# Up products of the first feed-forward read through 21 ways of laying out and addressing their operands

## The chip, the cores and the metric

The kernel runs on one core of a Trainium2 chip. The metric is the device time of one execution in microseconds, the median of several runs. Everything below on single instructions comes from one profiled execution of the kernel before.

## What is computed

A two-layer trunk over 256 tokens of width 2048. Layer 0 is differential attention and a gated feed-forward with a causal convolution; layer 1 is a gated DeltaNet and the same kind of feed-forward. The change touches the up products of the first feed-forward and, beside them, the two products in which the weights are the moving operand (the values of the attention, the gate z of the DeltaNet):

```python
def conv_ffn(h, w_up, conv_w, conv_b, w_down):
    u = causal_dwconv(h @ w_up, conv_w) + conv_b
    val, gate = jnp.split(u, 2, axis=-1)
    return (jax.nn.silu(gate) * val) @ w_down

for i in range(DEPTH):
    h = rms_norm(x, mixer_norm[i])
    x = x + (diff_attention(h, ...) if i % 2 == 0 else gated_deltanet(h, ...))
    x = x + conv_ffn(rms_norm(x, ffn_norm[i]), ffn_w_up[i], ffn_conv_w[i], ffn_conv_b[i], ffn_w_down[i])
```

`h @ w_up` is 256 x 2048 by 2048 x 11008, that is 43 blocks of 128 value and 128 gate columns.

## The kernel before, in words

All activations lie with features on the 128 partitions and tokens along the free dimension. A float32 number is carried as the sum of two float32r numbers, hi and lo, and a product is made of three: hi by hi, lo by hi, hi by lo. These are lines 115, 116 and 117 in `dense`. Each is one matmul with its own load of 128 x 128 weights; the activations move (256 columns), the weights stand still. `dense` makes one tile of 2 x 128 output features over all of the input features: 16 groups of 128 input features, two output halves (c), three products, which is 96 matmuls for a tile of 16 groups. The weights come in chunks of four groups: `weights` issues a DMA of 512 KB on SP (line 88), ScalarE rounds the chunk to float32r (line 89, tile `whi`), and VectorE takes the rest (line 90, tile `wlo`). `raw`, `whi` and `wlo` have three buffers each.

Where the operands lie matters to this text. `whi` and `wlo` have room for 128 columns more than they hold, and `weights` starts them `d` columns into that room. The activations stand at known places modulo 128 columns (512 bytes of a partition): the normed input `h` at 40, the feed-forward's inner activations `ac` at 48, the DeltaNet's `oc` at 112 (HP, AP, OP). `dense` passes d = (place - 45) mod 128, so that in every one of its products the weights stand 45 columns behind the activations modulo 128. Chunks, groups and halves are multiples of 128 columns, so they keep this distance.

`dense_tok` (line 139) turns the roles round: the activations are loaded as weights (128 tokens), the weight tile moves, 256 columns at a time, and d = (40 + 45) mod 128 keeps the same distance. It serves the attention's values (`w_v`, 4 calls) and the DeltaNet's z (`w_z`, 8 calls), with 192 matmuls a call.

Order of the work: attention, first feed-forward (43 up tiles in `ffn`, line 262, then the down products in `project`), DeltaNet, second feed-forward. Small products of the attention and the DeltaNet (lines 226, 475 to 658) are put between the chunks of the large ones. Each engine works through its queue in program order, and what waits for what is set by the tiles.

Of the kernel before, what the change touches and what calls it, by code (L numbers as in the profile page):

```python
# [16 lines left out]
P = 128  # L17
T = 256
D = 2048
KD = D // P  # L20
EPS = 1e-6
CK = 4
GAP = 45
HP, AP, OP = 40, 48, 112
LNEXP = "natural_log_exp_and_others"


class Trunk:
# [69 lines left out]
    def banks(self):  # L98
        return self.dps.tile([P, 2, 2 * T], F32, tag="ps", name="ps")

    def dense(self, w, kt, acts, place, tiles=2, lead=0):

        nc = self.nc
        ps = self.banks()
        for k0, nk in self.chunks(kt, CK, lead):
            hi, lo = self.weights(w[:, k0:k0 + nk, :], (place - GAP) % P)
            steps = [(k, c) for k in range(nk) for c in range(tiles)]
            if k0 + nk == kt:
                steps = [(k, c) for c in range(tiles) for k in range(nk)]
            for k, c in steps:  # L110
                a = acts(k0 + k)
                first, last = k0 + k == 0, k0 + k == kt - 1
                s = slice(c * P, (c + 1) * P)
                o = ps[:, c, :T]
                nc.tensor.matmul(o, hi[:, k, s], a[:, 0, :], start=first, stop=False)  # L115
                nc.tensor.matmul(o, lo[:, k, s], a[:, 0, :], start=False, stop=False)  # L116
                nc.tensor.matmul(o, hi[:, k, s], a[:, 1, :], start=False, stop=last)  # L117
            self.tick()
        return ps

# [1 line left out]

        self.nc.vector.tensor_tensor(u, ps[:, :, :T], self.rstd.unsqueeze(1).to_broadcast([P, 2, T]), ALU.mult)

    def dense_tok(self, w, kt, acts):

        nc = self.nc
        ps = self.banks()
        for k0, nk in self.chunks(kt, CK // 2):
            hi, lo = self.weights(w[:, k0:k0 + nk, :], (HP + GAP) % P)  # L130
            for k in range(nk):
                a = acts(k0 + k)
                first, last = k0 + k == 0, k0 + k == kt - 1
                for c in range(2):
                    ah, al = (a[:, i, c * P:(c + 1) * P] for i in range(2))
                    halves = [slice(i * T, (i + 1) * T) for i in range(2)]
                    for j, (l, r) in enumerate(((ah, hi), (ah, lo), (al, hi))):
                        for i, s in enumerate(halves):
                            nc.tensor.matmul(ps[:, c, s], l, r[:, k, s],  # L139
                                             start=first and not (i or j), stop=last and i + j == 3)  # L140
            self.tick()
        return ps
# [108 lines left out]
    def ffn(self, w_up, w_down, nj, cols_ap, done, final=False):  # L251

        nc = self.nc
        self.spawn(self.norm_stat())
        with self.tc.tile_pool(name="fp", bufs=1) as fp:
            cols = fp.tile([P, 8 * nj + 64], F32, tag="fcols", name="fcols")[:, :8 * nj]
            cols = cols.rearrange("p (t h j) -> p t h j", t=4, h=2)
            nc.scalar.dma_start(cols, cols_ap)
            acts = []
            rows = self.rows(fp.tile([P, nj * 2 * T + 8], F32R, tag="ac", name="ac"), nj, 0)  # L260
            for j in range(nj):
                ps = self.dense(w_up[j], KD, self.h_acts, HP)
                c = []
                u = fp.tile([P, 2, T], F32, tag="u", name="u", bufs=2)
                self.merge(ps, u)
                for half in range(2):
                    o = fp.tile([P, T], F32, tag=f"cv{half}", name="cv", bufs=2)
                    c4 = [cols[:, t, half, j:j + 1] for t in range(4)]
                    self.conv(o, u[:, half, :], c4[:3], c4[3])
                    c.append(o)  # L270
                nc.scalar.activation(c[1], c[1], AF.Silu)
                a = c[0]
                nc.vector.tensor_tensor(a, c[0], c[1], ALU.mult)
                ac = rows[j]
                self.split(ac, a)
                acts.append(ac)
            self.project(w_down, nj, lambda k: acts[k], AP, done, final)

    def attention(self, w_qk, w_v, w_o, nh, dist_ap, ident_ap, qg, kg, lvec, sub, start, done, lambda_init):

        nc, mp = self.nc, self.mp
        with self.tc.tile_pool(name="at", bufs=1) as at:
# [107 lines left out]
            for h in range(nh):  # L390
                acts, lead = (self.h_acts, 0) if h else (start, 1)
# [4 lines left out]
                self.spawn(weigh(h, qn, kn, go, aT))  # L396
                aTs.append(aT)
            for h in range(0, nh, 2):
                pv = self.dense_tok(w_v[h // 2], KD, self.h_acts)
                v = at.tile([P, 2, 2 * T], F32, tag="v", name="v", bufs=2)  # L400
                for c in range(2):
                    nc.scalar.mul(v[:, c, :], pv[:, c, :], self.rstdc[:, c:c + 1])
                for i in range(2):
                    self.spawn(values(h + i, v[:, :, i * T:(i + 1) * T], aTs[h + i]))
# [7 lines left out]
    def gdn(self, w_gate, w_in, w_z, w_out, nb, hb, gate_ap, const_ap, hot_ap, conv_col, ng, done):  # L412
# [7 lines left out]
        nc, tc, mp = self.nc, self.tc, self.mp  # L420
# [4 lines left out]
        with tc.tile_pool(name="gd", bufs=1) as gd:  # L425
# [25 lines left out]
            def convs(u, tiles):  # L451
                c = gd.tile([P, 2, T], F32, tag="cv", name="cv", bufs=4)
                for i in range(2):
                    self.conv(c[:, i, :], u[:, i, :], [conv_col(t, tiles[i]) for t in range(4)], None)
                nc.scalar.activation(c, c, AF.Silu)  # L455
                return c
# [213 lines left out]
            for b in range(nb):  # L670
                heads = range(b * hb, (b + 1) * hb)
                cc = gd.tile([P, 32, 32], F32, tag="s4", name="Cc", bufs=3)
                nc.gpsimd.memset(cc, 0.0)
                lqs, inv, acts, zts, vts = [], [], [], {}, {}
                groups = [range(i, i + gh) for i in range(0, hb, gh)]
                plan = [("k", i) for i in range(hb)] + [("v", 0)] + [("z", g) for g in range(len(groups))]
                for op, i in plan + [("v", i) for i in range(1, hb)]:
                    if op == "k":
                        hq = heads[i]
                        c = convs(lin(self.dense(w_in[hq * 2], KD, self.h_acts, HP)), (hq, nq + hq))  # L680
                        self.spawn(keys(hq, c, cc, 2 * i, lqs))
                        if i == hb - 1:
                            self.spawn(invert(cc, lqs, inv))
                    elif op == "z":
                        gr = groups[i]
                        zt = zts[i] = gd.tile([P, 2, gv, P], F32, tag="vz", name="zt", bufs=4)
                        ps = self.dense_tok(w_z[heads[gr[0]] // 2], KD, self.h_acts)
                        for t in range(2):
                            nc.scalar.activation(zt[:, t].rearrange(flat), ps[:, t, :], AF.Silu,
                                                 scale=self.rstdc[:, t:t + 1])  # L690
                    else:
                        gi = i // gh
                        gr = groups[gi]
                        if i == gr[0]:
                            vt = gd.tile([P, 2, gv, P], F32, tag="vz", name="vt", bufs=4)
                            ready = []
                            self.spawn(group(gi, gr, lqs, inv, vt, ready, zts, acts))
                        hq = heads[i]
                        c = convs(lin(self.dense(w_in[hq * 2 + 1], KD, self.h_acts, HP)),
                                  (2 * nq + 2 * hq, 2 * nq + 2 * hq + 1))  # L700
                        self.spawn(to_tokens(c, vt, 2 * (i - gr[0]), ready))
                if pend:
                    out(*pend)
                pend = (b, acts)
# [59 lines left out]
NJ = 43  # L764
# [5 lines left out]
def _tiles(a):  # L770

    return a.reshape(-1, P).T


def _layout(inputs):
# [3 lines left out]
    x = {k: np.asarray(v) for k, v in inputs.items()}  # L779
# [9 lines left out]
    def blocks(w, kt, starts):  # L789
        w = w.reshape(kt, P, -1)  # L790
        return np.stack([np.concatenate([w[:, :, a:a + n] for a, n in s], 2) for s in starts]).transpose(0, 2, 1, 3)

    def pairs(n):
        return [[(T * i, T)] for i in range(n)]
# [8 lines left out]
    up = [[(j * P, P), (ff + j * P, P)] for j in range(NJ)]  # L803
    q, k = np.arange(P)[:, None], np.arange(T)[None]
    dist = []
    for t, n in ((0, P), (1, T)):
# [3 lines left out]
    i = np.arange(P)  # L810
# [3 lines left out]
    fcols = [  # L814
        np.concatenate([_tiles(x["ffn_conv_w"][i].reshape(-1)), _tiles(x["ffn_conv_b"][i])], 1).reshape(P, 4, 2, NJ)
        for i in range(2)]
    out = {
        "x": x["x"][0].T.reshape(KD, P, T).transpose(1, 0, 2),
        "cols": np.concatenate(col, 1),
# [3 lines left out]
        "dist": np.concatenate(dist, 1),  # L823
        "fcols0": fcols[0],
        "fcols1": fcols[1],
        "w_up0": blocks(x["ffn_w_up"][0], KD, up),
        "w_down0": blocks(x["ffn_w_down"][0], NJ, pairs(D // T)),
        "w_gate": np.pad(wi[:, 2 * kd + 2 * vd:], ((0, 0), (0, P - 2 * NV))).reshape(KD, P, P).transpose(1, 0, 2),
        "w_in": blocks(wi, KD, gin),
# [78 lines left out]
```

## Time and profile before

| what | value |
|---|---|
| median of 3 runs | 2676.85 us (2675.2 to 2677.72) |
| the profiled execution: its own time | 2676.33 us |
| the profiled execution: span from first to last instruction | 2674.6 us |
| TensorE matmul busy | 2656.4 us, 99% of the span |
| VectorE, ScalarE, GpSimd busy | 69%, 54%, 4% |
| granted TensorE clock, mean | 0.999 |
| DMA | 481.77 MB, mean 180 GB/s |
| up products of the first feed-forward | from 405 to 874 us of the span |

How to read it: a matmul's row in the trace gives its start and a modelled duration of about 278 ns, in which the next two matmuls already start. The pace of TensorE is therefore not read from the duration but from start to start, or from the number of matmuls in a stretch of time. That pace is called the spacing below.

### The profile page before, as it was taken

To read this page: it belongs to the slowest core of one execution; us is meant where nothing else is said; L and a number is where in the kernel's file an instruction comes from. 1 tells how busy PE (TensorE), PEld (TensorE's weight loads), DVE (VectorE), ACT (ScalarE), POOL (GpSimd) and SP (SyncE) were. 2 spreads that over 40 slices of the span, in tenths; PEclk is the share of its full clock that TensorE was granted. 3 is DMA by queue.
4 is the path that set the end of the run, shared out by engine and by line. 5 is a ranking of instruction groups with operands and counts; after the bars stand their busy time and mean duration, and the time that the engine had idled before them with its cause. 6 is when DMAs were issued, how large, how long until landed. Compare 5 with 4: busy or idle time off the path is not lost.

```text
span 2674.6 us, 55978 instructions
## 1 busy us (share of the span) xinstructions
PE 2656.4 (99%) x23504; PEld 2639.4 (99%) x23504; DVE 1845.2 (69%) x2719; ACT 1453.3 (54%) x1994; POOL 112.1 (4%) x221
## 2 busy tenths in 40 slices
PE   8999999999999999999999999999999999999999
PEld 8999999999999999999999999999999999999999
DVE  7775567777777555688787687688677777776444
ACT  6555555555555444584764664574565555554333
POOL 0000000000000000031011021021000000000000
PEclk9999999999999999999999999999999999999999
DMA  6555566666666666655355454555466666666765
GB/s 205 172 174 164 159 192 194 195 195 193 195 193 195 193 194 192 190 156 177 115 170 166 143 169 155 157 159 174 143 194 195 194 193 196 193 195 197 203 200 165
DMA packets 135469, 481.77 MB, mean 180 GB/s; under 512 B 15408, under 2 KB 18480, under 8 KB 135216
## 3 DMA queue, kind: packets, MB, share of 16 engines
q1 hardware_dynamic: 134064, 475.58, 58.6%
q8 instruction: 184, 3.01, 0.5%
q10 hardware_dynamic: 1152, 2.61, 0.3%
q14 instruction: 69, 0.57, 0.1%
HBM read 476.03 MB, written 2.10 MB: 179 GB/s over the span
## 4 chain that ended last, share of the span: by engine, by line
PE 93%; DVE 3%; ACT 3%; issue 1%; DMA 1%; ACTq 0%; DVEq 0%; SPq 0%
PE ps L115 26%; PE ps L116 26%; PE ps L117 26%; PE ps L139 10%; PE mp L610 2%; DVE wlo L90 1%; ACT whi L89 1%; PE mp L226 1%; DVE cv L207 1%; ACT L455 0%; PE mp L574 0%; PE mp L580 0%; DMA raw<-w_in 0%; PE mp L589 0%; PE mp L498 0%
## 5 line engine op out<-in xcount | busy, mean ns | idle before, releaser
L90 DVE TENSOR_TENSOR wlo<-raw,whi 128x1024 fp32r<-128x1024 f32 (+2 forms) x909 | 1105.2, 1217 | 660.9 <-ACT whi L89 659.8
L89 ACT CAST whi<-raw 128x1024 fp32r<-128x1024 f32 (+2 forms) x909 | 948.6, 1044 | 1034.8 <-PE ps L117 830.8
L115 PE MATMUL ps<-h,whi 128*128 128x256 f32 x4304 | 1195.0, 278 | 7.8 <-ACT h L152 5.6
L116 PE MATMUL ps<-h,wlo 128*128 128x256 f32 x4304 | 1194.8, 278 | 4.4 <-DVE wlo L90 4.4
L117 PE MATMUL ps<-h,whi 128*128 128x256 f32 x4304 | 1193.7, 277 | 0.0
L115 PEld LDWEIGHTS ps<-h,whi 128*128 128x128 f32 x4304 | 809.4, 188 | 9.8 <-ACT h L152 5.6
L116 PEld LDWEIGHTS ps<-h,wlo 128*128 128x128 f32 x4304 | 809.8, 188 | 7.7 <-DVE wlo L90 5.9
L117 PEld LDWEIGHTS ps<-h,whi 128*128 128x128 f32 x4304 | 810.0, 188 | 0.6
L115 PE MATMUL ps<-ac,whi 128*128 128x256 f32 x1632 | 450.4, 276 | 0.0
L116 PE MATMUL ps<-ac,wlo 128*128 128x256 f32 x1632 | 450.3, 276 | 0.0
L117 PE MATMUL ps<-ac,whi 128*128 128x256 f32 x1632 | 450.2, 276 | 0.0
L115 PEld LDWEIGHTS ps<-ac,whi 128*128 128x128 f32 x1632 | 306.2, 188 | 0.0
L116 PEld LDWEIGHTS ps<-ac,wlo 128*128 128x128 f32 x1632 | 306.2, 188 | 0.0
L117 PEld LDWEIGHTS ps<-ac,whi 128*128 128x128 f32 x1632 | 306.2, 188 | 0.0
L139 PE MATMUL ps<-whi,h 128*128 128x256 f32 x1536 | 251.1, 284 | 0.0
L139 PEld LDWEIGHTS ps<-whi,h 128*128 128x128 f32 x1536 | 213.5, 190 | 0.2
L139 PE MATMUL ps<-wlo,h 128*128 128x256 f32 x768 | 155.7, 284 | 1.0 <-DVE wlo L90 1.0
L115 PE MATMUL ps<-oc,whi 128*128 128x256 f32 x512 | 143.9, 281 | 0.0
L207 DVE SCALAR_TENSOR_TENSOR cv<-u,fcols,cv 128x255 f32<-128x255 f32 (+1 forms) x344 | 142.8, 477 | 0.0
L117 PE MATMUL ps<-oc,whi 128*128 128x256 f32 x512 | 142.5, 278 | 0.0
L116 PE MATMUL ps<-oc,wlo 128*128 128x256 f32 x512 | 142.3, 278 | 0.0
L139 PEld LDWEIGHTS ps<-wlo,h 128*128 128x128 f32 x768 | 119.4, 190 | 2.0 <-DVE wlo L90 1.4
(201 smaller groups left out, 2048.7 us busy)
## 6 DMA issues: line engine op xcount, KB each, us to landing
raw<-w_up SPq DMA_DIRECT2D x344, 512.0 KB, 4.3
raw<-w_down SPq DMA_DIRECT2D x160, 512.0 KB, 4.1
raw<-w_in SPq DMA_DIRECT2D x128, 512.0 KB, 4.1
raw<-w_z SPq DMA_DIRECT2D x64, 512.0 KB, 4.4
raw<-w_out SPq DMA_DIRECT2D x64, 512.0 KB, 3.9
raw<-w_qk SPq DMA_DIRECT2D x63, 512.0 KB, 4.0
raw<-w_v SPq DMA_DIRECT2D x32, 512.0 KB, 3.7
raw<-w_o SPq DMA_DIRECT2D x32, 512.0 KB, 4.1
```

The costliest lines, as they stand in the source:

```text
L89: nc.scalar.copy(hi, raw)
L90: nc.vector.tensor_tensor(lo, raw, hi.bitcast(F32), ALU.subtract)
L115: nc.tensor.matmul(o, hi[:, k, s], a[:, 0, :], start=first, stop=False)
L116: nc.tensor.matmul(o, lo[:, k, s], a[:, 0, :], start=False, stop=False)
L117: nc.tensor.matmul(o, hi[:, k, s], a[:, 1, :], start=False, stop=last)
L139: nc.tensor.matmul(ps[:, c, s], l, r[:, k, s], start=first and not (i or j), stop=last and i + j == 3)
L207: nc.vector.scalar_tensor_tensor(out[:, j:], u[:, :T - j], taps[n - 1 - j], out[:, j:], ALU.mult, ALU.add)
L226: last = self.nc.tensor.matmul(out, self.onesr, p[:, j], start=i + j == 0, stop=i + j == n)
L610: nc.tensor.matmul(p[:, v, :], l(v), r[:, v, :], start=i == 0, stop=i == len(terms) - 1)
```

## The change

Nothing is added to or taken from any engine's queue: the changed program has the same instructions in the same order on every engine, with the same waits and the same bytes moved. What changes is where in memory some operands stand and in which order a matmul reads and writes their columns.

A table WAYS of 21 triples (unit, back, shift) is used in the first feed-forward alone; up tile j takes entry j mod 21.

- unit 1: the two halves of a weight tile are interleaved, column by column, when the input is laid out on the host. The load of half c then reads every second column (step of two columns, 8 bytes), 128 of 256.
- back 1: the moving activations are read from the last column to the first, and the output is written to PSUM from the last column to the first, so that the result is the same.
- shift: the weights start that many columns further on, so that their distance to the activations changes.

The entries are (0,0,0) once, (1,1,16i) and (1,0,16i) for i from 0 to 7, and (0,1,32i) for i from 0 to 3. Of the 43 tiles 3 keep (0,0,0), 16 are interleaved and backwards, 16 interleaved alone, 8 backwards alone.

In `dense_tok` the moving weights are shifted too: by 0, 11, 22 and 33 columns in the four calls of the values, and by 44, 55 and so on to 121 in the eight calls of z. One of these 12 calls keeps its place.

```diff
+WAYS = [(0, 0, 0)] + [(1, 1, 16 * i) for i in range(8)] + [(1, 0, 16 * i) for i in range(8)] + [
+    (0, 1, 32 * i) for i in range(4)]
...
-    def dense(self, w, kt, acts, place, tiles=2, lead=0):
+    def dense(self, w, kt, acts, place, tiles=2, lead=0, way=(0, 0, 0)):
...
+        unit, back, shift = way
+
+        def cols(t, k, c):
+            if not unit:
+                return t[:, k, c * P:(c + 1) * P]
+            return t[:, k, :].rearrange("p (g c u) -> p c g u", c=2, u=unit)[:, c]
+
+        def turn(t):
+            return t[:, ::-1] if back else t
+
         for k0, nk in self.chunks(kt, CK, lead):
-            hi, lo = self.weights(w[:, k0:k0 + nk, :], (place - GAP) % P)
+            hi, lo = self.weights(w[:, k0:k0 + nk, :], (place - GAP + shift) % P)
...
-                s = slice(c * P, (c + 1) * P)
-                o = ps[:, c, :T]
-                nc.tensor.matmul(o, hi[:, k, s], a[:, 0, :], start=first, stop=False)
-                nc.tensor.matmul(o, lo[:, k, s], a[:, 0, :], start=False, stop=False)
-                nc.tensor.matmul(o, hi[:, k, s], a[:, 1, :], start=False, stop=last)
+                o = turn(ps[:, c, :T])
+                nc.tensor.matmul(o, cols(hi, k, c), turn(a[:, 0, :]), start=first, stop=False)
+                nc.tensor.matmul(o, cols(lo, k, c), turn(a[:, 0, :]), start=False, stop=False)
+                nc.tensor.matmul(o, cols(hi, k, c), turn(a[:, 1, :]), start=False, stop=last)
...
-    def dense_tok(self, w, kt, acts):
+    def dense_tok(self, w, kt, acts, shift):
...
-            hi, lo = self.weights(w[:, k0:k0 + nk, :], (HP + GAP) % P)
+            hi, lo = self.weights(w[:, k0:k0 + nk, :], (HP + GAP + shift) % P)
...
-                ps = self.dense(w_up[j], KD, self.h_acts, HP)
+                ps = self.dense(w_up[j], KD, self.h_acts, HP, way=WAYS[j % len(WAYS)] if not final else WAYS[0])
...
-                pv = self.dense_tok(w_v[h // 2], KD, self.h_acts)
+                pv = self.dense_tok(w_v[h // 2], KD, self.h_acts, 11 * (h // 2))
...
-                        ps = self.dense_tok(w_z[heads[gr[0]] // 2], KD, self.h_acts)
+                        ps = self.dense_tok(w_z[heads[gr[0]] // 2], KD, self.h_acts, 44 + 11 * (heads[gr[0]] // 2))
...
+    ups = blocks(x["ffn_w_up"][0], KD, up)
+    for j in range(NJ):
+        u = WAYS[j % len(WAYS)][0]
+        if u:
+            ups[j] = ups[j].reshape(P, KD, 2, P // u, u).swapaxes(2, 3).reshape(P, KD, T)
...
-        "w_up0": blocks(x["ffn_w_up"][0], KD, up),
+        "w_up0": ups,
```

## The prediction

> **What bounds the kernel now.** I read the page first, its line of busy shares and the chain that ended last.
>
> ```profile
> PE 2656.4 (99%) x23504; PEld 2639.4 (99%) x23504; DVE 1845.2 (69%) x2719; ACT 1453.3 (54%) x1994; POOL 112.1 (4%) x221
> ...
> PE 93%; DVE 3%; ACT 3%; issue 1%; DMA 1%; ACTq 0%; DVEq 0%; SPq 0%
> PE ps L115 26%; PE ps L116 26%; PE ps L117 26%; PE ps L139 10%; PE mp L610 2%; DVE wlo L90 1%; ACT whi L89 1%; PE mp L226 1%; DVE cv L207 1%; ACT L455 0%; PE mp L574 0%; PE mp L580 0%; DMA raw<-w_in 0%; PE mp L589 0%; PE mp L498 0%
> ```
>
> TensorE has 93% of the chain, and nearly all of it is the four lines that the change touches. Next I read the groups of instructions in the stretch of the first feed-forward's up products alone, to see whether anything else could end last there.
>
> ```profile
> L116 PE MATMUL ps<-h,wlo 128*128 128x256 f32 x1376 | 379.9, 276 | 0.0
> ...
> L90 DVE TENSOR_TENSOR wlo<-raw,whi 128x1024 fp32r<-128x1024 f32 x172 | 210.8, 1226 | 114.9 <-ACT whi L89 114.9
> L89 ACT CAST whi<-raw 128x1024 fp32r<-128x1024 f32 x172 | 181.0, 1052 | 202.6 <-PE ps L117 173.1 <-ACT cv L205 26.6 <-DMA raw<-w_up 2.9
> ```
>
> The matmuls have no idle time before them (0.0). ScalarE, which makes the weight chunks, stands idle for 202.6 us, 173.1 of these waiting for matmuls to free a buffer; only 2.9 us are put down to the DMA. So the supply of weights is ahead, and the stage lasts exactly as long as its matmuls. The table of stretches gives their pace (us, then PE busy and its count, PEld, DVE, ACT, POOL):
>
> ```profile
> 405.20:873.90 468.70, 468.70 (x4136) 468.65 (x4135) 334.83 (x476) 256.65 (x347) 0.00 (x0) 1.00 0.64 194
> ```
>
> 468.70 us over 4136 matmuls is 113.3 ns each, at a granted clock of 1.00. This is the number that everything hangs on: a matmul moves 256 columns, and while it does, the 128 columns of the next weights are loaded. The timeline of TensorE shows that the same products, with the same three lines and the same distance between their operands, have another pace elsewhere. First a piece of this stage, then one of the DeltaNet's input products, then the products with moving weights:
>
> ```profile
> 499.76 0.28 PE L116 MATMUL ps<-h,wlo 128*128 128x256 f32 x1
> ...
> 500.44 0.28 PE L116 MATMUL ps<-h,wlo 128*128 128x256 f32 x1
> ```
> ```profile
> 1409.78 0.28 PE L116 MATMUL ps<-h,wlo 128*128 128x256 f32 x1
> ...
> 1411.94 0.28 PE L116 MATMUL ps<-h,wlo 128*128 128x256 f32 x1
> ```
> ```profile
> 1214.91 0.64 PE L139 MATMUL ps<-whi,h 128*128 128x256 f32 x4
> 1215.39 0.40 PE L139 MATMUL ps<-wlo,h 128*128 128x256 f32 x2
> ...
> 1217.07 0.64 PE L139 MATMUL ps<-whi,h 128*128 128x256 f32 x4
> ```
>
> In the first there are 6 matmuls from start to start in 0.68 us, 113.3 ns; in the second 18 in 2.16 us, 120.0 ns; in the third 6 in a group of 4 and 2, three groups, 18 in 2.16 us, again 120.0 ns. None of these waits for anything. So there is a second, slower pace, 6.7 ns a matmul away, and something that isn't a semaphore decides between the two. A cause that fits is that the two reads of TensorE, the moving columns and the weights, get into each other's way in the memory; the trace doesn't prove it.
>
> For the lowest price I looked for products whose two reads go side by side at one pace. The small float32 products of the DeltaNet do: 128 moving columns beside 128 columns of weights.
>
> ```profile
> 1284.72 0.94 PE L610 MATMUL mp<-vt,TT 128*128 128x128 f32 x7
> ```
> ```profile
> L610 PE MATMUL mp<-vt,TT 128*128 128x128 f32 x128 | 18.6, 278 | 0.0
> ```
>
> Seven of them end 0.94 us after the first has started, and one lasts 278 ns, so the spacing is (0.94 - 0.28) / 6 = 110 ns. A load of 128 weight columns therefore fits in 110 ns, and 113.3 has 3.3 ns over that.
>
> **The change part by part.** Order, waits and bytes stay, so no wait is added or removed, and DMAs, ScalarE and VectorE do what they did. Even at 110 ns a chunk of 24 matmuls would take 2.64 us, and VectorE, its busiest supplier, has 334.83 of 468.70 us to do in this stage, so no other engine becomes late. All that can move is the spacing of the 40 changed up tiles (96 matmuls each, 3840) and of the 11 changed calls with moving weights (192 each, 2112). One nanosecond on the first is 3.84 us, on the second 2.11 us.
>
> *Interleaved, forward: 16 tiles, 1536 matmuls.* The moving columns go by at twice the pace of the weight columns, 256 against 128. With a step of two columns the weights advance as fast in memory as the moving columns, and the distance between both reads stays what the shift makes it. No row shows a step of two. Bounds: 110 ns, the float32 products, where both also go at one pace, and 120 ns, the slow pace, where a bad distance would hold all the way. Eight distances in steps of 16 sample both kinds, and nothing in the rows says which is commoner; I take the middle, 115: 1536 x 1.7 = +2.6 us.
>
> The Trainium skill ("SBUF — State Buffer", "Door 1: The DMA port swizzle") has lines of 16 bytes that need two hits each for full bandwidth. A step of 8 bytes has just two hits in a line, so by that rule the load is not slower by itself; no run here shows it yet.
>
> *Backwards: 8 tiles not interleaved, 768 matmuls, and 16 interleaved, 1536.* Now both reads run towards each other. Taken modulo 128 columns (the period in which the kernel places its operands), the moving read overtakes the weights by 256 - 128 = 128 columns in a matmul now, once round; backwards it is 256 + 128, three times, and interleaved 256 + 256, four times. If one meeting costs the 3.3 ns that this stage has over 110, three cost 9.9 (120 ns, which is the slow pace) and four 13.2 (123.2 ns). If a meeting gets cheaper as it gets shorter, the cost stays at 113.3. I take the middle between the ends: 116.6 and 118.3, so 768 x 3.3 = +2.6 us and 1536 x 5.0 = +7.7 us. That the matmul also writes its output backwards is priced at nothing here; what it costs if that is wrong is the third rival.
>
> *Moving weights at other distances: 2112 matmuls.* They run at 120.0 now, with the distance at which the still weights run at 113.3. Bounds: 113.3, a gain of 2112 x 6.7 = 14.1 us, and one meeting more, 123.3, a loss of 7.0 us. They keep the slow pace at a distance that is good elsewhere, so distance alone doesn't seem to decide for them; I stay near the row of their own and let a quarter of them reach 113.3: -3.5 us.
>
> Sum: 2.6 + 2.6 + 7.7 - 3.5 = +9.4 us. The profiled execution took 2676.33 us by its own time (span 2674.6), 0.5 us below the median of 2676.85; 2676.3 + 9.4 = 2685.7, and I say 2686.
>
> **The rivals.** A measurement of this kernel can tell about 0.2%, 5.4 us, from no change.
>
> *Faster: reads that never meet.* Place: the 16 interleaved forward tiles and the calls with moving weights. If equal pace is what lets the float32 products run at 110, those tiles gain 1536 x 3.3 = 5.1 us, and if half of the moving-weight matmuls reach 113.3, 7.1 us more. It decides as long as the backward tiles stay at 113.3 to 114.5 (at most 2304 x 1.2 = 2.8 us): then 2676.3 - 12.2 + 1.4 = 2665.5 us. For it: the 110 of the float32 rows. Against it: float32 columns move at half the pace, so the memory has less to deliver there, and 24 of the 40 tiles run backwards. Chance 0.20.
>
> *Nothing happens.* If the two reads don't share anything, and 113.3 against 120.0 comes from how the matmuls are issued, then neither distance nor direction matters: 2676 us, within 0.2%. Against it: the two paces differ inside one stage's kind of product without any wait between. Chance 0.13.
>
> The Trainium skill ("TensorE: Matmul & The Clock Gate", "Step-by-step: what each phase is for") says just this: TensorE has two independent read ports, and loading the next weights takes no bandwidth from the running matmul. The two paces in the rows above speak against reading that as the whole story, but don't refute it.
>
> *One stream falls to half its pace.* In its first microseconds the kernel ran at such a pace:
>
> ```profile
> 10.08 0.42 PE L115 MATMUL ps<-h,whi 128*128 128x256 f32 x1
> ...
> 11.36 0.41 PE L115 MATMUL ps<-h,whi 128*128 128x256 f32 x1
> ```
>
> Six matmuls in 1.28 us are 213 ns. If columns written or read backwards went one at a time where two go together now, the 24 backward tiles would go at 213: 2304 x 100 = +230 us, 2907 us. If the step of two halved the load of weights, the 32 interleaved tiles would: 3072 x 100 = +307 us, 2984 us. For it: no row shows a negative or a wider step on TensorE at all. Against it: each pair of neighbouring columns is still read and written one after the other. Chance 0.17, most of it on the backward writes.
>
> The Trainium skill ("PSUM — Partial Sum Buffer", "Specifications (TRN2)") says that any access pattern that isn't contiguous slows matmuls significantly, with lines of 8 bytes. Whether a step of minus one counts as that it doesn't say; by the strict reading it would be this rival.
>
> **How the numbers follow.** The forecast's own case has 0.50: a few nanoseconds either way, the balance slower. Its ends: forward at 110 (-5.1), backward at 113.3 (0) and moving weights half at 113.3 (-7.1) make 2664; forward at 120 (+10.3), backward at 120 and 123.3 (+5.1 and +15.4), moving weights at 123.3 (+7.0) make 2714. The faster rival, at 2665.5, and the one in which nothing happens lie inside. The range from 2662 to 2716 thus leaves out the half-paced stream, 0.17, and some 0.03 on the fast side. Chances: slower by over 0.2% is the half pace, 0.17, and six sevenths of the forecast's case, 0.43, together 0.60; within 0.2% is nothing happens, 0.13, and the rest of the forecast's case, 0.07, together 0.20; faster 0.20.
>
> **What would show it.** In the profile after, the timeline of TensorE by tile: tile j begins about 10.9 us after tile j - 1 now. Tiles 1 to 8 and 22 to 29 (both) should be the slowest, tiles 9 to 16 and 30 to 37 (forward) should scatter about 115 with some near 110, tiles 17 to 20 and 38 to 41 (backwards) should lie between 113.3 and 120. The stage, 468.70 us before, should take about 482. The calls with moving weights should keep 120.0 in most cases. Idle time of the matmuls should stay 0.0 and the granted clock 1.00. I am wrong if any group runs near 213, if all tiles stay at 113.3, or if the tiles and stages that keep their layout (the down products behind this stage) fall to 120 because a slow pace, once taken up, is kept.

## The result and the profile after

The changed kernel takes 2690.91 us (median of 4 runs, 2690.76 to 2691.26) against 2676.35 us (4 runs): a ratio of 1.0054, 95% interval 1.0037 to 1.0072. It is slower by 14.6 us; the forecast was 2686.0, between 2662 and 2716.

The page of the kernel after has the same shares as before, and the lines of the up products (now L126 to L128) the same place in the chain; the line of busy shares and the first row of the chain:

```profile
PE 2670.4 (99%) x23504; PEld 2653.8 (99%) x23504; DVE 1848.7 (69%) x2719; ACT 1453.0 (54%) x1994; POOL 112.4 (4%) x221
...
PE 93%; DVE 3%; ACT 3%; issue 1%; DMA 1%; SPq 0%; DVEq 0%; ACTq 0%
```

The groups of instructions in the stretch of the first feed-forward's up products, of the kernel after:

```profile
L127 PE MATMUL ps<-h,wlo 128*128 128x256 f32 x1376 | 388.5, 282 | 0.0
...
L127 PEld LDWEIGHTS ps<-h,wlo 128*128 128x128 f32 x1376 | 266.8, 194 | 0.0
...
L91 ACT CAST whi<-raw 128x1024 fp32r<-128x1024 f32 x172 | 180.6, 1050 | 229.4 <-PE ps L128 196.8 <-ACT cv L216 32.6
```

The matmuls still wait for nothing (0.0), and ScalarE waits for them longer than before, 196.8 us where it was 173.1. So the stage is longer because TensorE is slower by itself. The table of stretches shows where. For the kernel after: the whole stage, tiles 1 to 8 (interleaved and backwards), 9 to 16 (interleaved, forward), 17 to 20 (backwards), and tile 21, which keeps its layout. Then the same stage of the kernel before and its tiles 1 to 8. Each stretch begins and ends where a tile begins, so its width over 96 matmuls a tile is the spacing.

```profile
404.88:894.93 490.05, 490.05 (x4137) 490.00 (x4136) 338.26 (x476) 256.38 (x347) 0.00 (x0) 1.00 0.60 186
416.70:507.38 90.68, 90.68 (x771) 90.68 (x769) 63.34 (x90) 48.68 (x65) 0.00 (x0) 1.00 0.60 186
507.38:599.27 91.89, 91.89 (x771) 91.89 (x770) 62.69 (x88) 47.38 (x64) 0.00 (x0) 1.00 0.59 184
599.27:644.91 45.64, 45.64 (x386) 45.64 (x385) 31.39 (x44) 23.69 (x32) 0.00 (x0) 1.00 0.60 185
644.91:655.81 10.90, 10.90 (x98) 10.90 (x97) 7.78 (x11) 5.93 (x8) 0.00 (x0) 1.00 0.61 189
```
```profile
405.20:873.99 468.79, 468.79 (x4137) 468.74 (x4136) 334.83 (x476) 256.65 (x347) 0.00 (x0) 1.00 0.64 194
417.02:504.06 87.04, 87.04 (x770) 87.04 (x769) 62.65 (x90) 48.71 (x65) 0.00 (x0) 1.00 0.64 194
```

Eight tiles took 87.04 us before, 113.3 ns a matmul. Now eight interleaved and backwards take 90.68 (118.1 ns), eight interleaved and forward 91.89 (119.7 ns), four backwards 45.64 (118.9 ns), and the unchanged one 10.90 (113.5 ns). The stage is 21.3 us longer, at a clock of 1.00.

That is more than the whole loss. The rest came back in two places. The calls with moving weights are 1.7 us shorter in all; the four of the values, with small products between, are the largest part of it (105.07 us before, 104.03 after). And 5.6 us came from products whose code and layout weren't touched: the DeltaNet's input products right behind a z call. The second of four such stretches, before and after:

```profile
1399.23:1433.78 34.55, 34.55 (x291) 34.55 (x289) 30.80 (x61) 16.57 (x20) 0.00 (x0) 1.00 0.58 183
```
```profile
1418.35:1451.04 32.69, 32.69 (x291) 32.69 (x289) 30.31 (x61) 16.68 (x20) 0.00 (x0) 1.00 0.60 191
```

The same 288 matmuls, 120.0 ns each before and 113.5 after. This stretch is the one in which the prediction had found the slow pace of 120.0. So 21.3 - 1.7 - 5.6 = 14.0 of the 14.6 us; the rest lies ahead of the attention's values, where nothing was changed, half of it before the first matmul.

### The profile page after: what moved, and what is told of

Same layout as the page of the kernel before. It is cut to its first block, busy times and chain, and to the rows that moved or that the text cites. A ratio compares the mean times of both kernels' runs of the same rounds, so it can differ in the third digit from the quotient of the medians.

```text
span 2689.2 us, 55978 instructions
## 1 busy us (share of the span) xinstructions
PE 2670.4 (99%) x23504; PEld 2653.8 (99%) x23504; DVE 1848.7 (69%) x2719; ACT 1453.0 (54%) x1994; POOL 112.4 (4%) x221
## 4 chain that ended last, share of the span: by engine, by line
PE 93%; DVE 3%; ACT 3%; issue 1%; DMA 1%; SPq 0%; DVEq 0%; ACTq 0%
PE ps L126 26%; PE ps L127 26%; PE ps L128 26%; PE ps L150 10%; PE mp L621 2%; DVE wlo L92 1%; ACT whi L91 1%; DVE cv L218 1%; PE mp L237 1%; ACT L466 0%; PE mp L585 0%; PE mp L591 0%; DMA raw<-w_in 0%; PE mp L600 0%; PE mp L665 0%
## 5 line engine op out<-in xcount | busy, mean ns | idle before, releaser
L126 PE MATMUL ps<-h,whi 128*128 128x256 f32 x4304 | 1202.8, 280 | 8.4 <-ACT h L163 6.0
L128 PE MATMUL ps<-h,whi 128*128 128x256 f32 x4304 | 1202.5, 279 | 0.0
L126 PEld LDWEIGHTS ps<-h,whi 128*128 128x128 f32 x4304 | 818.5, 190 | 10.2 <-ACT h L163 6.0
L127 PEld LDWEIGHTS ps<-h,wlo 128*128 128x128 f32 x4304 | 818.8, 190 | 7.6 <-DVE wlo L92 5.9
L128 PEld LDWEIGHTS ps<-h,whi 128*128 128x128 f32 x4304 | 818.8, 190 | 0.6
L126 PE MATMUL ps<-ac,whi 128*128 128x256 f32 x1632 | 451.3, 277 | 0.0
L128 PE MATMUL ps<-ac,whi 128*128 128x256 f32 x1632 | 451.2, 277 | 0.0
L126 PEld LDWEIGHTS ps<-ac,whi 128*128 128x128 f32 x1632 | 306.5, 188 | 0.0
L128 PEld LDWEIGHTS ps<-ac,whi 128*128 128x128 f32 x1632 | 306.4, 188 | 0.0
L126 PE MATMUL ps<-oc,whi 128*128 128x256 f32 x512 | 144.2, 282 | 0.0
L128 PE MATMUL ps<-oc,whi 128*128 128x256 f32 x512 | 142.8, 279 | 0.0
```

Of the source, the lines that this page charges most:

```text
L126: nc.tensor.matmul(o, cols(hi, k, c), turn(a[:, 0, :]), start=first, stop=False)
L127: nc.tensor.matmul(o, cols(lo, k, c), turn(a[:, 0, :]), start=False, stop=False)
L128: nc.tensor.matmul(o, cols(hi, k, c), turn(a[:, 1, :]), start=False, stop=last)
```

## The experiments

All are built on the changed kernel. Where the way of the up products isn't named, it is (0, 0, 0), and where the shift of the moving weights isn't named, it is 0. In the first experiment the moving weights keep the shifts of the changed kernel.

**The moving weights alone.**

```diff
-WAYS = [(0, 0, 0)] + [(1, 1, 16 * i) ...]
+WAYS = [(0, 0, 0)]
```

> The shifts of the moving weights alone; the up products of the first feed-forward as before. In the changed kernel the calls with moving weights took 1.7 us less than before, and the stretches of DeltaNet input products behind them 5.6 us less. Theory 'a slow pace is kept': the distance in a call with moving weights also decides at which pace the products behind it begin; then both gains come here too, 2676.35 - 7.3 = 2669.0 us (ratio 0.9973), and the 21.3 us of the up products are gone. Rival: the 5.6 us behind the calls came from the changed first feed-forward or from chance in the timing; then only the 1.7 us stay, 2674.7 us.

Measured: 2668.62 us (9 runs) against 2675.47, a ratio of 0.9975, interval 0.9965 to 0.9985. The stretch behind the z call, of this kernel:

```profile
1395.90:1428.59 32.69, 32.69 (x291) 32.69 (x289) 30.49 (x61) 16.68 (x20) 0.00 (x0) 1.00 0.60 191
```

It is as short as in the kernel after, with the first feed-forward as it was. So the two halves of the change add up, 21.3 us lost and some 7 gained, and the pace behind a z call depends on where that call's weights lay. That a slow pace is kept until something disturbs it fits this, and the kernel before shows such an end. Its third stretch behind a z call runs at 120.0 until 32 small matmuls (line 553) come in between at 1634.90 us, and at 113.3 behind them. The first row below is 16 matmuls wide, the second 9:

```profile
1632.77:1634.69 1.92, 1.92 (x19) 1.92 (x17) 1.92 (x3) 0.30 (x1) 1.84 (x3) 1.00 0.04 11
1635.98:1637.00 1.02, 1.02 (x12) 1.02 (x10) 0.96 (x3) 0.66 (x3) 0.90 (x3) 1.00 0.91 313
```

The slow piece has hardly any DMA beside it (share 0.04, the last number but one) and the fast one much (0.91), so the transfers aren't what makes these matmuls slow. What keeps a pace isn't seen.

**Shift alone, read straight and forward.**

```diff
+WAYS = [(0, 0, 3 * i) for i in range(43)]
```

> Up tile j of the first feed-forward reads straight and forward, with the weights shifted by 3j columns (0 to 126); moving weights as before. Theory 'meeting reads': the distance between the two reads of TensorE sets the pace, so the tiles scatter between 113.3 and 124 ns a matmul, the mean near 118 as in the changed tiles, about +19 us, 2695 us. Rival 'pattern': the step of two columns and the step of minus one cost 4 to 7 ns by themselves, and a straight read has 113.3 ns at every distance: 2676 us.

Measured: 2695.02 us (one run). The stage, then tiles 30 to 32 (shifts 90, 93, 96) and tiles 33 and 34 (99, 102) of this kernel:

```profile
403.85:892.50 488.65, 488.65 (x4136) 488.60 (x4135) 337.99 (x476) 256.80 (x347) 0.00 (x0) 1.00 0.60 186
746.16:778.83 32.67, 32.67 (x291) 32.67 (x290) 23.32 (x33) 17.80 (x24) 0.00 (x0) 1.00 0.61 192
778.83:801.85 23.02, 23.02 (x194) 23.02 (x193) 15.70 (x22) 11.85 (x16) 0.00 (x0) 1.00 0.60 186
```

32.67 us for 288 matmuls is 113.4 ns, 23.02 for 192 is 119.9. Three columns further is all that lies between. Only five of the 43 shifts have 113.3: 0, 3, 90, 93 and 96; the others lie between 115.7 and 121.8. The place of the weights counts by itself, without any step of two or minus one, and the stage with 43 shifts of the old layout lasts about as long (488.65 us) as the changed stage (490.05).

**Reading and writing backwards apart.**

```diff
+WAYS = [(0, i, 0) for i in (0, 1, 2, 3)]
...
-                o = turn(ps[:, c, :T])
+                o = turn(ps[:, c, :T], 2)
```

`turn(t, b)` reverses where `back & b`, with b = 1 for the activations read and 2 for the output written.

> Up tile j by j mod 4: as before; activations read backwards but the output written forwards; read forwards but written backwards; both backwards. In the second and third kind the token order of these features comes out reversed. Theory 'meeting reads': the cost lies in the reading; read backwards 117 to 120 ns a matmul like both backwards, written backwards 113.3. Rival 'PSUM': the cost lies in writing the output against the direction of its lines; written backwards 117 to 120, read backwards 113.3. In both cases 21 or 22 of the 43 tiles are slow, about +11 us, 2687 us.

Measured: 2688.61 us (one run). Tiles 1 to 4, read backwards, written backwards, both, neither:

```profile
415.81:427.33 11.52, 11.52 (x98) 11.52 (x97) 8.42 (x13) 7.31 (x9) 0.00 (x0) 1.00 0.58 183
427.33:438.25 10.92, 10.92 (x99) 10.92 (x98) 7.80 (x11) 5.93 (x8) 0.00 (x0) 1.00 0.62 188
438.25:449.76 11.51, 11.51 (x98) 11.51 (x97) 7.85 (x11) 5.93 (x8) 0.00 (x0) 1.00 0.60 186
449.76:460.68 10.92, 10.92 (x99) 10.92 (x97) 7.80 (x11) 5.93 (x8) 0.00 (x0) 1.00 0.63 191
```

Writing backwards takes what the unchanged tile takes, 10.92 us. Reading backwards takes 11.52, 120.0 ns a matmul, and both together no more. The rival that blamed PSUM falls, at the one distance that this run has.

**Interleaved and forward at every distance.** Two kernels: shifts 0 to 42 in the first feed-forward; then 43 to 85 in the first and 86 to 128 in the second. In the first of them the second feed-forward's up products are read in steps of two as well, without their weights being laid out so, which mixes its values; its total holds two slow stages.

```diff
+WAYS = [(1, 0, i) for i in range(43)]
```

> All 43 up tiles interleaved and read forward, tile j shifted by j columns (0 to 42, every single column where the changed kernel had every sixteenth). Theory 'meeting reads': both reads advance at the same speed in memory, so the distance stays, and some of the fine distances should be free of clashes and reach 110 to 113.3 ns while others stay at 120; mean 115 to 118. Rival 'pattern': a step of two columns costs by itself; all tiles at 119 to 120 ns, 4128 x 6.3 = +26 us, 2702 us.

> Interleaved weights read forward at the distances not yet tried: shifts 43 to 85 in the first feed-forward and 86 to 128 in the second, whose weights are laid out interleaved too. Theory 'pattern of two': nowhere below 118, mean 120 as for the shifts 0 to 42, twice about 28 us more, 2731 us. Theory 'equal pace can pass without a clash': some distances at 110 to 113.3.

Measured: 2731.1 and 2731.4 us (one run each). 42 tiles of a stage (4032 matmuls) of the first kernel, and of it the tile with shift 41:

```profile
416.50:901.08 484.58, 484.58 (x4034) 484.58 (x4033) 330.02 (x464) 250.58 (x337) 0.00 (x0) 1.00 0.58 183
...
878.37:889.73 11.36, 11.36 (x99) 11.36 (x98) 7.85 (x11) 5.93 (x8) 0.00 (x0) 1.00 0.58 186
```

and of the second kernel the tile with shift 105:

```profile
2215.28:2226.64 11.36, 11.36 (x99) 11.36 (x97) 7.85 (x11) 5.92 (x8) 0.00 (x0) 1.00 0.60 185
```

The mean is 120.2 ns. The fastest tile (shift 41, 11.36 us, 118.3) and the slowest (shift 25, 122.2) come back 64 columns further on, at 105 and 89. So distance counts here too, with a period of 64 columns that only shifts 1 and 2 miss (120.0 and 119.0 against 118.6 and 118.4), but no distance gives less than 118.3. The theory that reads of one pace could pass each other without a clash falls.

**Backwards at 43 distances, and both together at 43 distances.**

```diff
+WAYS = [(0, 1, 3 * i) for i in range(43)]
```

and the same with (1, 1, 3 * i).

> All 43 up tiles read and written backwards, tile j shifted by 3j columns. Theory 'place and distance' without anything special in the step of minus one: some distances at 113.3, as for the forward reads, where 9 of 43 shifts lay below 117; mean 118. Rival 'backwards costs': nothing below 117.7, the value of two of the four distances tried; mean 119, +23 us, 2699 us.

> All 43 up tiles interleaved and backwards, tile j shifted by 3j columns. In the changed kernel six of the eight such distances had 117.8 and two 118.9. Theory 'here both reads keep their distance': nearly all at 117.8, with few distances apart, so that what is paid is the step of two and not a meeting; mean 118, +19 us, 2695 us. Rival 'distance counts here too, and sixteens hid it': a scatter from 113.3 to 123 as for the straight reads.

Measured: 2697.62 and 2697.02 us (one run each). 42 tiles of the first and of the second kernel:

```profile
416.41:895.62 479.21, 479.21 (x4034) 479.21 (x4033) 329.99 (x464) 249.94 (x337) 0.00 (x0) 1.00 0.58 185
```
```profile
416.12:894.29 478.17, 478.17 (x4034) 478.17 (x4032) 330.00 (x464) 249.95 (x337) 0.00 (x0) 1.00 0.58 185
```

Backwards has a mean of 118.9 and tiles from 117.8 to 120.0: nothing below, as the rival said. Both together have 118.6, about half the tiles at 117.8 and a few up to 123.2, so neither theory was quite right there: the distance does count, but again no tile is under 117.7.

Read beside the straight reads, this says more than either theory. At the same 42 shifts the straight tiles have a mean of 118.3 ns, backwards 118.9, both 118.6, interleaved and forward 120.1; at 16 of the 42 shifts the backward tile is even the faster one. So on the mean of the distances a layout costs between 0.3 and 1.8 ns. What all three lack is the few places at 113.3, and the kernel before stood at one of these.

**Place or distance.** The normed input and its weights are moved together.

```diff
-HP, AP, OP = 40, 48, 112
+HP, AP, OP = 43, 48, 112
...
-        self.place(0)
+        self.place(3)
```

> The normed input and the weights beside it are both moved by 3 columns, so that their distance stays as it was and only their places change. Theory 'distance': up products at 113.3 ns in both feed-forwards and about 2676 us. Rival 'places': what counts is where each read begins in the memory's lines, and the pace of the up products changes to 117 or 120 ns: twice 4128 x 3.7 to 6.7 ns, 2706 to 2730 us.

Measured: 2706.19 us (one run). 42 tiles of the first feed-forward, and a steady piece of a z call, of this kernel:

```profile
417.32:892.08 474.76, 474.76 (x4033) 474.76 (x4032) 329.96 (x464) 250.17 (x337) 0.00 (x0) 1.00 0.60 187
```
```profile
1229.99 0.39 PE L149 MATMUL ps<-wlo,h 128*128 128x256 f32 x2
...
1232.71 0.39 PE L149 MATMUL ps<-wlo,h 128*128 128x256 f32 x2
```

The same distance, 45 columns, three columns further along, and the up products go at 474.76 / 4032 = 117.7 ns. The products with moving weights, whose distance is the same too, do the opposite: 24 matmuls in 2.72 us, 113.3 ns where it was 120.0. One call of the values begins at 120.0 in this kernel too, and goes over to 113.3 behind small products. So distance alone isn't the cause; the place counts as well. The read that moves went from a multiple of 4 columns to three past one in the first case (40 to 43), and from one past to a multiple of 4 in the second (85 to 88).

**Looking for a better place for the moving weights.** Four kernels: every call at shift 22; the twelve shifts 16 to 27; every call at shift 35; and one place a call.

```diff
-                pv = self.dense_tok(w_v[h // 2], KD, self.h_acts, 11 * (h // 2))
+                pv = self.dense_tok(w_v[h // 2], KD, self.h_acts, 22)
```

> All 12 calls with moving weights shifted by 22 columns, the distance that had the fastest steady pace of the eleven (117.0 ns a matmul against 120.0); the up products as before. Theory 'distance decides in each call, and the products behind it start at the pace it leaves': 12 calls x 192 x 3.0 ns = 6.9 us, and some 5 us in the input products behind the z calls, 2675.5 - 12 = 2663.5 us. Rival: 117.0 belonged to that one call of the values and not to its distance; then the z calls stay at 120 and the gain is about that of the eleven distances, 2668.6 us or less of it.

> The moving weights shifted by 16 to 19 columns in the four calls of the values and by 20 to 27 in the eight of z. Theory 'distance': paces between 113.3 and 123 ns that change from one column to the next, as with the still weights, and 117.0 again at 22 although that is now a call of z. Rival 'alignment': paces repeat with the position in a line, every fourth column alike.

> All 12 calls with moving weights shifted by 35 columns, which puts the weights at column 120 modulo 128, a multiple of 8 as the normed input at 40 is, at a distance of +48 to the activations, in the middle of the second good stretch of the straight reads (+45 to +51). Theory 'place of the moving read and distance both count': 113.3 ns a matmul, 2304 x 6.7 = 15.4 us, and some 5 us behind the z calls, 2675.3 - 20.4 = 2655 us. Rival 'these calls have their own good distances': 117 to 120 as at the eleven others, 2663 to 2675 us.

> The moving weights at places that are multiples of 4 or 8 columns, one a call: values at 84, 88, 80 and 120, z at 116, 84, 88, 124, 120, 96, 112 and 0. Theory 'place and distance': 113.3 at 84 (distance -44) and at 120 (distance +48), slower at 96, 112 and 0, which lie outside the good distances; 88 and 80 are beside them. Rival 'place alone': all multiples of 8 at 113.3, whatever the distance.

Measured, shift 22: 2663.39 us (5 runs) against 2675.3, ratio 0.9953, interval 0.9939 to 0.9967. A steady piece of a z call:

```profile
1210.22 0.39 PE L149 MATMUL ps<-wlo,h 128*128 128x256 f32 x2
...
1213.03 0.39 PE L149 MATMUL ps<-wlo,h 128*128 128x256 f32 x2
```

24 matmuls in 2.81 us, 117.1 ns, in z as in the values: at this shift the pace belongs to the place, not to the call. The shifts 16 to 27 (2668.27 us, one run) show how fine the dependence is. Steady pieces at shift 23, 24 and 25 of this kernel:

```profile
1380.69 0.40 PE L149 MATMUL ps<-wlo,h 128*128 128x256 f32 x2
...
1383.49 0.40 PE L149 MATMUL ps<-wlo,h 128*128 128x256 f32 x2
...
1566.88 0.41 PE L149 MATMUL ps<-wlo,h 128*128 128x256 f32 x2
...
1567.62 0.43 PE L149 MATMUL ps<-wlo,h 128*128 128x256 f32 x2
...
1590.65 0.40 PE L149 MATMUL ps<-wlo,h 128*128 128x256 f32 x2
...
1593.53 0.40 PE L149 MATMUL ps<-wlo,h 128*128 128x256 f32 x2
```

They are 116.7 ns (24 in 2.80 us), 123.3 (6 in 0.74) and 120.0 (24 in 2.88). The paces of the twelve shifts come back nearly every four columns. The moving weights begin 85 columns further on than the shift. Over stretches of 24 matmuls with nothing in between, the median pace of a call is 123.1 to 123.3 where that place is one past a multiple of 4, 120.0 two past, 117.0 to 120.0 three past, and 116.7 to 120.0 on a multiple of 4. The rival "alignment" was nearer the truth here than my theory. It isn't the whole truth: in the kernel after, the calls one past have 120.0, 120.8 and 123.3, and those two past 120.0, 120.8 and 120.0. The place of before, 85, is one past and has 120.0.

Nor does a multiple of 4 suffice. Shift 35, place 120, gave 2664.10 us (5 runs; ratio 0.9955, interval 0.9941 to 0.9968) and mostly 117.8 ns, not the 113.3 I expected from the good distances of the still weights. But some of its calls begin at 113.3. The second call of the values, before and behind eight pairs of small products (lines 383 and 384):

```profile
232.63:237.39 4.76, 4.76 (x45) 4.76 (x43) 2.21 (x2) 3.23 (x4) 0.00 (x0) 1.00 0.47 129
240.70:242.82 2.12, 2.12 (x20) 2.12 (x19) 1.32 (x2) 1.18 (x2) 0.00 (x0) 1.00 0.69 195
```

The first row is 42 matmuls wide, 113.3 ns, the second 18, 117.8 ns, in one call with its operands at the same places. So a place can have two paces, and small products in between can end one as well as the other. The multiples of 4 and 8, one a call (2665.0 us, one run), show it again: both calls at 88 and one of the two at 120 go at 113.3 in parts and at 117.8 in others, and the other calls have median paces from 116.7 (112) to 120.0 (0 and 124). With the input at 43, as above, the calls at 88 go nearly all the way at 113.3. Shifts 22 and 35 aren't told apart by their times; both are faster than the kernels before and after.

## Why the prediction was right

*What bounds the stage.* Right: no wait came or went, and the loss is all spacing.

*Interleaved and backwards*, forecast 118.3 ns and +7.7 us: measured 118.1 and 2 x (90.68 - 87.04) = +7.3 us. The size was right, but not for the reason given, meetings of one fixed price. Had that been right, the tiles that read forward without a step of two would all cost the same whatever the shift, and they don't.

*Backwards alone*, forecast 116.6 and +2.6 us: measured 118.9 and +4.2 us, the upper part of the bounds. That the backward writes cost nothing was right at the distance that was tried.

*Interleaved and forward*, forecast 115 and +2.6 us: measured 119.7 and 2 x (91.89 - 87.04) = +9.7 us. This is the term that failed most, and with it the order: the tiles with both were to be the slowest, and the forward ones are. I took the middle between the float32 products' 110 and the slow pace, as if the distances came in two kinds. No distance has the pace of the float32 products; the step of two never went below 118.3. The float32 products move their columns at half the speed, which I had named as the reason against them and then weighed at half.

*Moving weights*, forecast -3.5 us: measured -1.7.

*What I had left out:* -5.6 us in the DeltaNet's input products behind the z calls. The row at 1409.78, with 120.0 for products that have 113.3 elsewhere, was in the prediction, and it stood right behind a z call. It could have been read as a pace that the call before had set; I read it only as a second pace that exists.

The sum of the terms was +9.4; with the measured terms it is 7.3 + 4.2 + 9.7 - 1.7 - 5.6 = +13.9. So the total came out near partly by luck, through two errors that partly cancel: 7.1 us too little for the forward tiles and 5.6 us left out. What carried the sign was sound: the 113.3 of before was near the lowest pace on record and 120.0 was known beside it, so a new place for the up tiles had more to lose than to gain.

*The rivals.* "Reads that never meet" falls with the 128 distances of the forward tiles. "Nothing happens" falls with the shifts alone. The Trainium skill's rule behind it ("TensorE: Matmul & The Clock Gate", "Step-by-step: what each phase is for"), that loading the next weights takes no bandwidth from the running matmul, isn't the whole story here: the pace goes from 113.3 to 121.8 with the weights' place alone. The rows of the weight loads don't show how: with the shifts alone they last 188 ns as before, and backwards too; with the step of two they are longer, 197 ns in the kernel with shifts 0 to 42 and 194 on the mean of the kernel after. "Half the pace" falls: no changed tile ran near 213. There the trace agrees with the Trainium skill's rule on lines of 16 bytes ("SBUF — State Buffer", "Door 1: The DMA port swizzle") in so far as a step of 8 bytes doesn't halve the load, though it isn't free. And a step of minus one in PSUM didn't slow the matmuls: 10.92 us a tile either way, so the strict reading that the prediction named doesn't hold here.

What stays open is the mechanism. That the two reads disturb each other fits what was seen, but no run takes one of the reads away, and it doesn't say why the same operands go at two paces, before and behind small products. In the up tiles the place decides nearly alone: each of the 20 ways of the kernel after has, within 0.1 ns, the same pace in its two tiles, 21 apart. That the moving read is best begun on a multiple of 4 columns is a tendency: place 107, three past one, has 117.0, and the multiples 104, 124 and 0 have 120.0. Nor was it tried to let the normed input stand at 43, where the moving weights have 113.3, with its still weights at a distance that is good for that place.

## What to carry to other kernels

When TensorE is busy all the time and waits for nothing, compare the spacing of equal matmuls in different stages: a difference of a few per cent is a cost that no view of waits names. It can be moved by where operands stand modulo 128 columns: survey the places of each pair of reads, many in one kernel, multiples of 4 float32r columns for the moving operand first, since a distance that is good for one pair wasn't for another. When a layout is judged, compare it over many places: at a single one the place can hide what the layout costs. A gain or a loss can also show up in untouched products behind the ones that were changed.

## What the runs showed of the hardware that I had not expected

- In the up tiles the place of the weights alone, in float32r with 256 moving columns, sets the spacing between 113.3 and 121.8 ns, and 3 columns can decide.
- Moving both operands by 3 columns, at the same distance, made one kind of product slower (113.3 to 117.7) and another faster (120.0 to 113.3); the pace of moving weights comes back nearly every four columns (123.1, 123.3 and 123.3 at shifts 16, 20 and 24).
- Reading the moving operand backwards costs 6.7 ns a matmul at the place of before (120.0 against 113.3), but only 0.6 on the mean of 42 places (118.9 against 118.3); writing the output backwards costs nothing at the place of before.
- With a load of weights in steps of two columns the tiles have 118.3 to 122.2 ns a matmul at the 126 distances read off whole tiles, 5 to 9 above the best straight place and 1.8 above the mean of the straight ones, with a pattern that comes back after 64 columns.
- Products behind a call keep or leave a slow pace according to how the call before them lay: 34.55 against 32.69 us for the same 288 matmuls. One call with its operands in place had 113.3 ns before some small products and 117.8 behind them.
